# Two pairs of rooms for the readout matrices, and the skip weights added once at the end

## Chip, core and metric

The kernel runs on one core of a Trainium2 chip, in float32. The metric is the device time of one execution in microseconds (us). Each engine (PE for matrix products, DVE and ACT for elementwise work, POOL for elementwise work and the DMAs it issues, SP for the other DMAs) works through its own queue strictly in the order of that queue; between engines, instructions wait for one another through semaphores.

## What is computed

Two layers over 256 latent and 256 context tokens, width 1024. Layer 0 is attention and then a mixture of experts (MoE); layer 1 is a state-space mixer (SSM) in both directions, a gated linear unit and a second MoE; a final norm ends it. The change lies in the preparation of the SSM:

```
lbar = exp((a_re + i a_im) * dt)                  # 2 directions x 64 groups x 64 states
bb   = (lbar - 1) / (a_re + i a_im) * b           # input matrices, 16 channels a group
state_t = lbar * state_(t-1) + bb u_t             # both directions
y = Re(c . state), forward + backward             # readout matrices c
out = glu(gelu(y + d * u))                        # d: skip weights, one a channel
```

The kernel scans over chunks of four tokens. So it needs, for each group, `W` (powers of `lbar` times `bb`), readout matrices (powers of `lbar` times `c`, for the four places of a chunk) and within-chunk matrices (what the tokens of one chunk give to one another, to which the skip weights are added on the diagonal). All of these depend on weights alone.

## The kernel before

**Where the matrices are built.** `ssm_matrices` is a generator. It is run in slices ("asides") inside the expert loop of the first MoE, which streams 96 MB of expert weights. That loop goes over 16 pairs of experts, in steps: step k turns the gathered rows of pair k (`rows`: PE transposes at L329, copies to `xgT` at L1232 by ACT and DVE; POOL gathers the next pair's rows, L1180), turns the hidden values of pair k-2 (`hidT`, PE L1237, DVE copy to `hT` L1239), takes one aside, multiplies pair k-1 up (L1251, then `sg` on ACT L1259 and `hd` on DVE L1260) and pair k-2 down (L1277, ACT L1279, POOL L1280). The weights come in 1 MB tiles on SP's queue (L186). From step 4 on they go round eight tiles, and a tile is loaded again when PE has used it.

**What an aside does.** The 64 groups are taken eight at a time, q = 0 to 7, one a step (steps 4 to 11; the last matrices come in step 12). In the code's order an aside i is: `mats(i-1)`, `loadB(i+1)`, `coef(i)`, `readout(i)`, `loadC(i+1)`.

- `coef(q)` makes `W` on DVE: 13 operations with line L149, which is the line of the helper `InOrder`.
- `readout(q)` makes the readout matrices on DVE (L1607, L1608, L1609; twice each, for r = 0 and 1) and sends them with two DMAs on POOL's queue (L1611) to `Rd` in memory, whence they are fetched in layer 1. The result of r = 0 lies in `rooms[0]`, a half of `H1` (`H` in the profile), that of r = 1 in `rooms[1]`, a half of `b2` (`b`). The same two rooms serve every q. `cells` holds the `c` of two turns; it is loaded at L1578.
- `mats(q)` transposes `W` on PE (L1621, copied by ACT at L1623), multiplies it with `C` (`kp`, L1630), copies and transposes the product (`kt` L1633, `pk` L1635), and evacuates `pk` into `Kd`: one direction by ACT (L1638), the other by DVE with the skip weights `db` added (L1639).

**What sets the order.** A scheduler puts each engine's queue in order ahead of the run, by its own estimate of when each instruction can start; an instruction that stands later in the code can thus stand earlier in its queue. The operations called through `VP_` (all of `coef`) are tied, by the first lines quoted here, to stand behind the DVE instruction that precedes them in the code:

```
for p in reversed(nc.cur_bb.bb.instructions):
    if p is not i and p.engine == i.engine:
        tc.add_manual_dep(i, p.name, ...)
...
TE_ = InOrder(nc.tensor, 1)
P_, VP_, A_ = InOrder(nc.gpsimd, 3), InOrder(nc.vector, 1), InOrder(nc.scalar, 1)
```

For the first operation of `coef(i)` that is the addition L1639 of `mats(i-1)`. The operations of `readout` (`V_`) are not tied.

**Afterwards.** Later asides (steps 13 to 15) build the within-chunk matrices out of `Kd` with DMAs and POOL operations, and `shift` writes a few rows into `brow` by a DMA on SP's queue and has PE transpose them (L1545). `brow` is a tile of 128x512 that holds bias rows in attention and again in layer 1. The tile with the tag `gb` is another of that size, used for norm gains at the same places.

Of the kernel before, what the change touches and what calls it, by code (L numbers as in the profile page):

```python
# [10 lines left out]
F32 = mybir.dt.float32  # L11
# [119 lines left out]
def bc(ap, shape):  # L131
    return ap.to_broadcast(shape)
# [3 lines left out]
def hybrid(ctx: ExitStack, tc: tile.TileContext, A, out, taps=None, stop=None):  # L136
    nc = tc.nc
    taps = taps or {}
    V_ = nc.vector
# [29 lines left out]
    sm = ctx.enter_context(tc.tile_pool(name="sm", bufs=1))  # L169
# [3 lines left out]
    def bank(tag="b", name="bank"):  # L173
        return psp["p"].tile([128, 512], F32, tag=tag, bufs=psp[tag], name=name)
# [46 lines left out]
    brow = per.tile([128, 512], F32, name="brow")  # L221
# [52 lines left out]
    Rd = dram.tile([128, 2, 64, 64], F32, name="Rd")  # L274
# [529 lines left out]
    def dispatch_open(layer, Ht, M, VB, tag, xn2=None):  # L804
# [50 lines left out]
        def st(name, shape, dt=F32, bufs=1):  # L855
            return dp.tile([128] + list(shape), dt, tag=name, bufs=bufs, name=name)

        def logits(t):
            turn(HT[t % 2], Ht[t], 1)
            pl = bank(name="pl")  # L860
            for kk in range(8):
                for i in range(nt):
                    p = slice(64 * i, 64 * i + 64) if nt == 2 else slice(0, 128)
                    nc.tensor.matmul(pl[p, :36], lhsT=HT[t % 2][:, kk, p], rhs=rws[:, kk, i], start=kk == 0, stop=kk == 7)
            L = lr[:, 360 + 36 * t:396 + 36 * t] if layer else st("L", [36], bufs=2)
            V_.scalar_tensor_tensor(L, in0=pl[:, :36], scalar=xns[t], in1=C, op0=OP.mult, op1=OP.add)
            xns[t] = L
            if layer == 0 and t >= 2:
                nc.gpsimd.memset(M.xg[t % 2], 0.0)

        def choose(t):
            L = xns[t]
            gl, el = L[:, 0:4], L[:, 4:36]

# [651 lines left out]
    def cmul(eng, o, x, y, tm, neg=False):  # L1526

        eng.tensor_mul(tm[0], x[0], y[0])
        eng.tensor_mul(tm[1], x[1], y[1])
        eng.tensor_sub(o[0], tm[0], tm[1])  # L1530
        eng.tensor_mul(tm[0], x[0], y[1])
        eng.tensor_mul(tm[1], x[1], y[0])
        eng.tensor_add(o[1], tm[0], tm[1])
        if neg:
            eng.tensor_scalar(o[1], o[1], -1.0, 0.0, op0=OP.mult, op1=OP.add)
# [13 lines left out]
    def ssm_matrices(sctx):  # L1549
# [4 lines left out]
        Kd = H1[:, 0].rearrange("p (d g c) -> p d g c", d=2, c=16)  # L1554
        with ExitStack() as bctx:
            with ExitStack() as wctx:
                wq = wctx.enter_context(tc.tile_pool(name="ssmw", bufs=1))
                st = {}

                db = H1[:, 1, 0:512].rearrange("p (g c) -> p g c", c=16)  # L1560
                for h in range(2):
                    nc.gpsimd.dma_start(db[64 * h:64 * h + 64].rearrange("p g c -> p (g c)"),
                                        A["sd"][h:h + 1].to_broadcast([64, 512]))
                eye = wq.tile([128, 16], F32, name="eye")
                nc.gpsimd.tensor_add(eye, ident[:, 48:64], ident[:, 112:128])


                rooms = [t.rearrange("p (g t c) -> p g t c", t=4, c=16) for t in (H1[:, 1, 512:1024], b2[:, 512:1024])]
                cells = b2[:, 0:512].rearrange("p (i r g c) -> p i r g c", i=2, r=2, c=16)
                cb = M0[0].oh.rearrange("p a b c -> p (a b c)").rearrange("p (r g c) -> p r g c", r=2, c=16)  # L1570
                tm = [wq.tile([128, NG, 4, 16], F32, name=f"tm{i}") for i in range(2)]
                Bs, Cs = {}, {}

                def loadB(q):
                    if q < 64 // NG:
                        Bs[q] = wq.tile([128, 2, NG, 16], F32, tag="B", bufs=2, name="B")
                        nc.gpsimd.dma_start(Bs[q], A["sbq"][q])
                        nc.gpsimd.dma_start(cells[:, q % 2], A["sc"][:, :, q * NG:q * NG + NG, :])  # L1578

                def loadC(q):  # L1580
                    if q < 64 // NG:
                        Cs[q] = wq.tile([128, 2, NG, 32], F32, tag="C", bufs=2, name="C")
                        nc.gpsimd.dma_start(Cs[q], A["scq"][q])
                loadB(0)
                loadC(0)


                def coef(q):
                    gs = slice(q * NG, q * NG + NG)
                    B, C = Bs.pop(q), Cs.pop(q)  # L1590
                    VP_.tensor_scalar(C[:, 1], C[:, 1], -1.0, 0.0, op0=OP.mult, op1=OP.add)
                    W = wq.tile([128, 2, NG, 4, 16], F32, tag="W", bufs=2, name="W")
                    st[q] = C, W
                    cmul(VP_, (cb[:, 0], cb[:, 1]), [bc(CF[:, i, gs][:, :, None], [128, NG, 16]) for i in range(2)],
                         (B[:, 0], B[:, 1]), [t[:, :, 0, :] for t in tm])
                    cmul(VP_, (W[:, 0], W[:, 1]),
                         [bc(LX[:, :, i, gs].rearrange("p t g -> p g t")[:, :, :, None], [128, NG, 4, 16]) for i in range(2)],
                         [bc(cb[:, i][:, :, None, :], [128, NG, 4, 16]) for i in range(2)], tm)

                def readout(q):  # L1600

                    gs = slice(q * NG, q * NG + NG)
                    C = [bc(cells[:, q % 2, i][:, :, None, :], [128, NG, 4, 16]) for i in range(2)]
                    L = [bc(LR[:, :, i, gs].rearrange("p t g -> p g t")[:, :, :, None], [128, NG, 4, 16]) for i in range(2)]
                    for r in range(2):
                        x, y = rooms[r], tm[r]
                        V_.tensor_mul(x, L[0], C[r])  # L1607
                        V_.tensor_mul(y, L[1], C[1 - r])  # L1608
                        V_.tensor_tensor(x, x, y, op=OP.add if r else OP.subtract)  # L1609
                    for r in range(2):  # L1610
                        nc.gpsimd.dma_start(Rd[:, r, gs], rooms[r].rearrange("p g t c -> p g (t c)"))  # L1611

                def mats(q):
                    C, W = st.pop(q)
                    g0 = q * NG // 2
                    for i in range(0, NG // 2, 2):
                        pt = bank("vt", name="vt")
                        for k in range(2):
                            for r in range(2):
                                g = 2 * (i + k)  # L1620
                                nc.tensor.transpose(pt[:, (2 * k + r) * 128:(2 * k + r) * 128 + 128],  # L1621
                                                    W[:, r, g:g + 2].rearrange("p g a b -> p (g a b)"), ident)
                        nc.scalar.copy(VR[:, g0 + i:g0 + i + 2], pt.rearrange("p (k r b) -> p k r b", k=2, r=2))  # L1623

                    kp = bank("kp", name="kp")
                    for h in range(2):
                        for r in range(2):
                            for i in range(NG // 2):
                                g = 2 * i + h
                                nc.tensor.matmul(kp[32 * i:32 * i + 32, 64 * h:64 * h + 64], lhsT=C[:, r, g, :],  # L1630
                                                 rhs=W[:, r, g].rearrange("p a b -> p (a b)"), start=r == 0, stop=r == 1)
                    kt = wq.tile([128, 128], F32, tag="kt", bufs=1, name="kt")
                    nc.scalar.copy(kt, kp[:, 0:128])  # L1633
                    pk = bank("vt", name="pk")
                    nc.tensor.transpose(pk[:, 0:128], kt, ident)  # L1635
                    pd = pk[:, 0:128].rearrange("p (i d c) -> p d i c", d=2, c=16)
                    gs = slice(g0, g0 + NG // 2)
                    nc.scalar.copy(Kd[:, 1, gs], pd[:, 1])  # L1638
                    V_.tensor_add(Kd[:, 0, gs], pd[:, 0], db[:, gs])  # L1639
                n = 64 // NG  # L1640
                for i in range(n + 1):
                    if i:
                        mats(i - 1)
                    if i < n:
                        loadB(i + 1)
                        coef(i)
                        readout(i)
                        loadC(i + 1)
                        if not i:
                            nc.gpsimd.tensor_mul(db, db, bc(eye[:, None, :], [128, 32, 16]))  # L1650
                        yield
            yield

            sp2 = sctx.enter_context(tc.tile_pool(name="ssm2", bufs=1))
# [447 lines left out]
```

## Time and profile before

| what | value |
|---|---|
| median of three runs | 1202.22 us (1200.32 to 1202.37) |
| the profiled execution | 1193.77 us, span of its instructions 1192.0 us |
| PE, DVE, ACT, POOL busy in the span | 912.6, 625.3, 349.5, 268.6 us |
| expert loop of the first MoE | about 401 to 712 us of the span |
| asides with `coef`, `readout` and `mats` | 443 to 588 us of the span |

Lines are those of the kernel; H and b are the rooms. "Idle before" or "waited for" is time in which an engine had nothing to do until the named releaser was done. PEclk is the granted clock of PE as a share of 2.4 GHz; the DMA share is the mean busy share of the 16 DMA engines. A wait behind which a busy engine or a full DMA queue stands costs nothing by itself.

### The profile page before, as it was taken

What the parts mean: (1) busy time and instruction counts of PE and PEld (TensorE: products, weight loads), DVE (VectorE), ACT (ScalarE), POOL (GpSimd) and SP (SyncE); (2) the same over time, 40 slices, a digit from 0 to 9 for tenths busy, and PEclk for the clock granted to TensorE, in tenths of its full rate; (3) what the DMA queues carried; (4) which work ended last, traced back from release to release, by engine and by line L of the source; (5) the groups of instructions that cost most, each with busy time, mean ns of one, the idle gap of its engine ahead of it and who ended that gap; (6) DMA issues with size and microseconds to landing.
All of it is one profiled execution on the core that took longest, in us unless ns stands there. A gap on an engine that the chain in (4) does not pass through costs nothing. (4 is left out here: it accounts for less than half of the span.)

```text
span 1192.0 us, 15041 instructions
## 1 busy us (share of the span) xinstructions
PE 912.6 (77%) x5398; PEld 477.6 (40%) x5398; DVE 625.3 (52%) x1656; ACT 349.5 (29%) x705; POOL 268.6 (23%) x347
## 2 busy tenths in 40 slices
PE   3587989999897599676897896975189597676763
PEld 0375865444486333222342244732068442122110
DVE  1778794676549425555510028989947841111113
ACT  2332225666533212111220113622763320000001
POOL 0533331322324323121116305010035300000001
PEclk7788999999998699978999997987589798777896
DMA  9782222666744689978899974374257679999993
GB/s 287 267 214 71 71 71 71 213 230 222 269 170 194 226 336 410 416 270 304 334 422 350 409 302 142 143 283 156 97 198 272 247 318 420 420 420 419 420 420 142
DMA packets 54814, 317.14 MB, mean 266 GB/s; under 512 B 8587, under 2 KB 9627, under 8 KB 21712
## 3 DMA queue, kind: packets, MB, share of 16 engines
q1 hardware_dynamic: 42910, 285.49, 63.3%
q0 software_dynamic: 10080, 26.92, 6.1%
q10 hardware_dynamic: 1746, 3.73, 0.9%
q8 instruction: 44, 0.72, 0.2%
q14 instruction: 34, 0.28, 0.1%
HBM read 305.80 MB, written 19.94 MB: 273 GB/s over the span
## 5 line engine op out<-in xcount | busy, mean ns | idle before, releaser
L1251 PE MATMUL ph<-w,xgT 128*64 128x512 f32 x512 | 134.8, 640 | 9.6 <-DMA w<-in_gu 9.6
L248 PE MATMUL pm<-wmod,cs 128*32 128x512 f32 x352 | 51.8, 681 | 61.7 <-DMA wmod<-in_modw 53.5
L339 PE MATMUL pp<-wlo,xo 128*128 128x512 f32 (+1 forms) x224 | 88.5, 395 | 4.9 <-POOL wlo L360 4.8
L338 PE MATMUL pp<-whi,xo 128*128 128x512 f32 (+1 forms) x224 | 90.5, 405 | 1.3 <-ACT whi L358 1.3
L340 PE MATMUL pp<-whi,xo 128*128 128x512 f32 (+1 forms) x224 | 87.9, 393 | 0.0
L1277 PE MATMUL py<-w,hT 128*64 128x512 f32 x224 | 73.7, 623 | 5.2 <-DMA w<-in_dn 5.0
L1251 PEld LDWEIGHTS ph<-w,xgT 128*64 128x64 f32 x512 | 38.7, 144 | 82.5 <-issue 57.7
L360 POOL TENSOR_TENSOR wlo<-win,whi 128x1024 fp32r<-128x1024 f32 (+1 forms) x20 | 44.9, 2265 | 78.8 <-ACT whi L358 78.8
L1251 PE MATMUL ph<-w,xn 128*32 128x512 f32 x256 | 42.4, 747 | 24.7 <-DMA w<-in_gu 24.6
L1260 DVE TENSOR_TENSOR a<-a,ph 128x256 f32<-128x256 f32 x8 | 3.4, 421 | 98.8 <-ACT a L1259 98.8
L1260 DVE TENSOR_TENSOR hd<-sg,ph 128x256 f32<-128x256 f32 x16 | 6.7, 418 | 86.7 <-ACT sg L1259 86.7
L1303 PE MATMUL py<-w,m 128*32 128x512 f32 x256 | 43.8, 778 | 9.7 <-DMA w<-in_dn 8.5
L339 PEld LDWEIGHTS pp<-wlo,xo 128*128 128x128 f32 x224 | 44.8, 200 | 15.1 <-POOL wlo L360 7.3
L338 PEld LDWEIGHTS pp<-whi,xo 128*128 128x128 f32 x224 | 44.9, 201 | 10.2 <-ACT whi L358 2.2
L582 DVE TENSOR_REDUCE nm<-sc 128x1 f32<-128x512 f32 (+1 forms) x64 | 35.0, 551 | 26.1 <-PE sc L615 15.5
L340 PEld LDWEIGHTS pp<-whi,xo 128*128 128x128 f32 x224 | 44.4, 198 | 8.8
L248 PEld LDWEIGHTS pm<-wmod,cs 128*32 128x32 f32 x352 | 9.4, 116 | 89.6 <-issue 51.3
L1003 DVE SCALAR_TENSOR_TENSOR Yl<-py,WS,Yh 128x512 fp32r<-128x512 f32 x18 | 13.4, 750 | 56.2 <-ACT Yh L1002 43.5
L1251 PE MATMUL ph<-w,xg 128*32 128x512 f32 x256 | 33.2, 649 | 12.3 <-DMA w<-in_gu 11.0
L1259 ACT ACTIVATE sg<-ph 128x256 f32<-128x256 f32 x16 | 6.1, 383 | 124.0 <-PE ph L1251 122.3
L363 POOL TENSOR_TENSOR wlo<-glu,whi 128x512 fp32r<-128x512 f32 x16 | 26.7, 1697 | 67.5 <-ACT whi L358 65.1
L585 ACT ACTIVATE e<-sc,nm 128x512 f32<-128x512 f32 (+1 forms) x64 | 37.4, 586 | 12.7 <-DVE nm L582 8.4
(486 smaller groups left out, 1964.0 us busy)
## 6 DMA issues: line engine op xcount, KB each, us to landing
w<-in_gu SPq DMA_DIRECT2D x127, 1024.0 KB
w<-in_dn SPq DMA_DIRECT2D x62, 1024.0 KB
wmod<-in_modw SPq DMA_DIRECT2D x42, 1024.0 KB
win<-in_win SPq DMA_DIRECT2D x8, 1024.0 KB
glu<-in_glu SPq DMA_DIRECT2D x8, 1024.0 KB
yd<-in_zero SPq DMA_DIRECT2D x1, 4096.0 KB
wo<-in_wout SPq DMA_DIRECT2D x4, 1024.0 KB
w<-yd SPq DMA_DIRECT2D x4, 1024.0 KB
```

What stands on the lines that cost most here:

```text
L248: nc.tensor.matmul(pm[32 * i:32 * i + 32, :], lhsT=cs[:, kk, :], rhs=w(kk), start=kk < 4, stop=kk >= 4)
L338: nc.tensor.matmul(o, lhsT=lh, rhs=rh, start=start, stop=False)
L339: nc.tensor.matmul(o, lhsT=lh, rhs=rl, start=False, stop=False)
L340: nc.tensor.matmul(o, lhsT=ll, rhs=rh, start=False, stop=stop)
L360: self.engines[i].tensor_tensor(lw, w[:, 2 * i:2 * i + 2, :], hi.bitcast(F32), op=OP.subtract)
L363: e.tensor_tensor(lw[:, k], w[:, 2 * i + k, :], hi.bitcast(F32)[:, k], op=OP.subtract)
L582: V_.tensor_reduce(nm, sp_[:, :n], axis=AX.X, op=OP.max, negate=True)
L585: nc.scalar.activation(e[:, :n], sp_[:, :n], AF.Exp, bias=nm, scale=1.0, accum_out=z)
L1003: V_.scalar_tensor_tensor(Yl[:, s], in0=py, scalar=ws, in1=Yh[:, s].bitcast(F32), op0=OP.mult, op1=OP.subtract)
L1251: nc.tensor.matmul(ph[s, :], lhsT=st["x"][:, 4 * q + kk, s], rhs=g[:, i, kk % 2] if M.dma else g[:, i], start=(q, kk) == (0, 0), stop=(q, ...
L1277: nc.tensor.matmul(py[s, :], lhsT=st["hT"][:, fk, s], rhs=d[i][:, fk, hf * 512:hf * 512 + 512], start=fk == 0, stop=fk == 1)
L1303: nc.tensor.matmul(py[s, :], lhsT=st["hT"][:, fk, s], rhs=r, start=fk == 0, stop=fk == 1)
```

## The change

The readout matrices get a second pair of rooms: `brow` and a new tile `Rr` with the tag `gb`. Even q use the first pair, odd q the second. And ACT evacuates both directions of `pk` at once, without the skip weights; these are added to all 32 entries of `Kd[:, 0]` by one DVE operation after the last `mats`.

```
+                rooms += [t.rearrange("p (g t c) -> p g t c", t=4, c=16)
+                          for t in (brow, sm.tile([128, 512], F32, tag="gb", bufs=1, name="Rr"))]
...
+                    o = rooms[2 * (q % 2):2 * (q % 2) + 2]
                     for r in range(2):
-                        x, y = rooms[r], tm[r]
+                        x, y = o[r], tm[r]
                         V_.tensor_mul(x, L[0], C[r])
                         V_.tensor_mul(y, L[1], C[1 - r])
                         V_.tensor_tensor(x, x, y, op=OP.add if r else OP.subtract)
                     for r in range(2):
-                        nc.gpsimd.dma_start(Rd[:, r, gs], rooms[r].rearrange("p g t c -> p g (t c)"))
+                        nc.gpsimd.dma_start(Rd[:, r, gs], o[r].rearrange("p g t c -> p g (t c)"))
...
-                    nc.scalar.copy(Kd[:, 1, gs], pd[:, 1])
-                    V_.tensor_add(Kd[:, 0, gs], pd[:, 0], db[:, gs])
+                    nc.scalar.copy(Kd[:, :, gs], pd)
...
                         yield
+                V_.tensor_add(Kd[:, 0], Kd[:, 0], db)
             yield
```

## Rows read from the trace of the kernel before

**Rows 1.** Chain that ended last, in order of time: start us, us, what.
```profile
964.27 16.77 DMA w<-in_dn
...
1141.91 19.89 DMA w<-in_gu
```

**Rows 2.** Windows: stretch, its us, busy us (x count) by engine, PEclk, DMA share, GB/s.
```profile
440.00:520.00 80.00, 65.95 (x400) 26.05 (x396) 43.83 (x94) 15.96 (x33) 20.22 (x28) 0.94 1.01 409
520.00:600.00 80.00, 61.97 (x357) 23.67 (x358) 44.34 (x91) 14.37 (x31) 16.01 (x21) 0.89 0.80 293
600.00:700.00 100.00, 84.85 (x346) 29.99 (x345) 10.64 (x19) 13.57 (x23) 33.31 (x70) 0.98 1.02 394
```

**Rows 3.** Waits of DVE from 440 to 600 us: total us, times, longest.
```profile
DVE H L1607 <- DMA Rd<-H: 32.0, 6, 7.9
DVE H L1639 <- ACT H L1638: 16.5, 4, 6.7
...
DVE b L1607 <- DMA Rd<-b: 4.2, 5, 1.4
```

**Rows 4.** Waits of PE in the same stretch.
```profile
PE vt L1621 <- DVE W L149: 24.7, 8, 8.3
```

**Rows 5.** Timeline of the longest PE wait: start us, us, engine, instruction, [idle before].
```profile
533.46 0.60 POOL L1611 DMA_DIRECT2D Rd<-H  x1
...
536.36 0.22 DVE L1639 TENSOR_TENSOR H<-pk,H 128x64 f32<-128x64 f32 x1 [6.73 <-ACT H L1638]
...
542.60 0.69 DVE L1607 TENSOR_TENSOR H<-LR,b 128x512 f32<-128x512 f32 x1 [5.42 <-DMA Rd<-H]
...
548.00 0.45 PE L1621 MATMUL vt<-cst,W 128*128 128x128 f32 x1 [8.35 <-DVE W L149]
```

**Rows 6.** Timeline of PE: transposes that open steps 4, 8, 11 and 12.
```profile
441.58 1.09 PE L329 MATMUL pt<-cst,xg 128*128 128x128 f32 x8
...
518.76 1.09 PE L329 MATMUL pt<-cst,xg 128*128 128x128 f32 x8
...
595.35 1.09 PE L329 MATMUL pt<-cst,xg 128*128 128x128 f32 x8
...
607.09 1.09 PE L329 MATMUL pt<-cst,xg 128*128 128x128 f32 x8
```

**Rows 7.** Groups by line, 440 to 600 us: shape, count, busy us, mean ns, idle before.
```profile
L1621 PE MATMUL vt<-cst,W 128*128 128x128 f32 x64 | 12.6, 301 | 25.4 <-DVE W L149 24.7 <-ACT Vm L1623 0.4
...
L1630 PE MATMUL kp<-W,C 128*32 128x64 f32 x256 | 8.4, 240 | 0.0
...
L1609 DVE TENSOR_TENSOR H<-H,tm 128x512 f32<-128x512 f32 x8 | 5.5, 683 | 0.0
...
L1635 PE MATMUL pk<-cst,kt 128*128 128x128 f32 x8 | 2.6, 329 | 2.7 <-ACT Vm L1623 2.7
...
L1633 ACT COPY kt<-kp 128x128 f32<-128x128 f32 x8 | 2.1, 267 | 0.3 <-PE kp L1630 0.3
...
L1639 DVE TENSOR_TENSOR H<-pk,H 128x64 f32<-128x64 f32 x8 | 1.8, 220 | 16.5 <-ACT H L1638 16.5
```

**Rows 8.** Line L1611, the 16 DMAs to Rd: time from issue to landing.
```profile
DMA to landing us min/median/max: 4.2/8.5/11.0
```

**Rows 9.** Timeline of DVE: L1607 hoisted, and `coef` against the `hT` copy.
```profile
401.13 0.69 DVE L1607 TENSOR_TENSOR H<-LR,b 128x512 f32<-128x512 f32 x1 [1.94 <-DVEq L1047]
...
460.39 0.69 DVE L1607 TENSOR_TENSOR H<-LR,b 128x512 f32<-128x512 f32 x1 [7.87 <-DMA Rd<-H]
...
560.29 0.41 DVE L1239 COPY hT<-pt 128x256 f32<-128x256 f32 x1
```

**Rows 10.** Timeline near the last matrices: POOL, PE, DVE.
```profile
586.12 0.57 POOL L1611 DMA_DIRECT2D Rd<-b  x1
...
589.85 0.27 PE L1545 MATMUL bt<-cst,brow 64*128 64x64 f32 x1
...
594.17 0.42 DVE L1260 TENSOR_TENSOR hd<-sg,ph 128x256 f32<-128x256 f32 x1 [5.61 <-ACT sg L1259]
```

## The prediction

> **What bounds the kernel now.** The chain that ended last comes first. From 964 us to the end it consists of weight loads of the second MoE, some 20 us a link [rows 1]. It says what holds the last fifth; what lies before it is shifted as a whole if an earlier stage ends sooner, since those loads begin only when the SSM's last part asks for them. So the question is whether the first MoE, where the changed code runs, ends sooner.
>
> The windows tell what bounds that stage [rows 2]. From 440 to 520 us and from 600 to 700 us the DMA share is 1.01 and 1.02: transfers bound it, and no engine can make it faster there. From 520 to 600 us the share is 0.80 with 293 GB/s instead of 409: 0.20 x 80 = 16 us of the transfer time are lost. Loads stop when no tile of the ring has been freed, and PE frees them. So PE is late there, although it is not at its limit: it is busy 62 of 80 us, at a granted clock of 0.89.
>
> Why PE is late: its largest wait is for `W`, made by DVE, 24.7 us in 8 waits [rows 4]. And DVE's own waits in this stretch are of the kinds that the diff touches [rows 3]: 36.2 us (32.0 + 4.2) at L1607, where the next readout may not write into a room before the DMA out of it has landed, and 16.5 us at L1639, which waits for PE and ACT to finish the matrices of the turn before. Together 52.7 us. Both stand in DVE's queue ahead of `coef` or within it, so `W` comes late. The longest case shows the whole chain [rows 5]: L1639 ends 6.73 us of idling at 536.36; the DMA issued at 533.46 holds L1607 until 542.60, a further 5.42 us, with most of `coef` behind it; PE gets its `W` at 548.00 after 8.35 us of nothing. The transpose behind the wait takes 0.45 us against a mean of 0.30 [rows 5, 7], so the lower clock after the idling makes PE later still.
>
> **The change, part by part.**
>
> *Two pairs of rooms.* L1607 of turn i now has to wait for the DMA of turn i-2. Its 16 DMAs land 4.2 to 11.0 us after issue, 8.5 at the median [rows 8]; a turn takes 19.3 us or more (below). If L1607 stays where it is in the code's order, the 36.2 us go to nothing. The bound on the other side is 36.2 us kept: L1607 is not tied to its place, and the trace shows it far ahead, at 401.13, four steps before its aside, and at 460.39 ahead of the copies of step 5, as soon as the scheduler thinks the room free [rows 9]. With two pairs it can be put one turn further ahead and stand at the same wait. I take the larger part as gone or harmless: even where L1607 of turn i+2 stands in front of the next step's copies, it is no longer in the middle of a `coef` that is already due.
>
> The Trainium skill ("DMA: Bandwidth & Descriptors", section "Anatomy of one DMA — SWDGE (gpsimd) path") gives such a transfer 2.0 us plus its bytes over 436 GB/s, an estimated 2.6 us for these 256 KB. By that figure the rooms would be free almost at once, and a second pair would save next to nothing. The trace does not agree: 8.5 us at the median, with the transfer engines full [rows 8, 2].
>
> *The addition L1639.* Eight DVE operations of 0.22 us go (1.8 us), and with them 16.5 us of waiting. Added are one DVE operation of 128x512 (as L1609: 0.68 us) and, on ACT, a copy twice as wide; the 128x128 copy `kt` takes 0.27 us, so all eight together cost less than 2.1 us [rows 7]. ACT is busy 14.4 us of the 80 [rows 2], which hides it. The new addition waits for the last copy as the last L1639 did, near 588 us; behind it DVE has nothing until `hd` at 594.17 [rows 10]. Without that cover it costs its 0.68 us once.
>
> *What is moved.* The first operation of `coef(i)` was tied behind L1639 of the matrices before; now the nearest DVE instruction ahead of it in the code is the `hT` copy of its own step. It can no longer run ahead of its step. Before, it could: `coef` of turn 5 followed L1639 at 536.36, while the `hT` copy of that step came at 560.29 [rows 5, 9]. Price: nothing, if `W` comes before PE reaches the matrices; at most a wait like the longest, 8.35 us, in each of eight steps.
>
> *The borrowed tiles.* `brow` is written by `shift` through SP's queue. That write must now follow the last DMA out of `brow`, issued at 586.12 and landing by 597 at the latest; PE used its result at 589.85, so this step moves back some 8 us [rows 8, 10]. Nobody needs it before layer 1, but SP's weight loads stand behind it: 0 us while loads already issued keep the transfer engines full, at most 11 us if none are. I take 0, since the share is 1.02 after 600 us [rows 2]. `gb` has no other user until layer 1.
>
> *The sum.* Two ways. First, the lost transfer time: 16 us, if PE frees tiles in time throughout. Second, the pace: steps 4 to 8 took 518.76 - 441.58 = 77.2 us with the transfers full, 19.3 us a step; steps 8 to 12 took 607.09 - 518.76 = 88.3 us [rows 6]. At the first pace the saving is 11.1 us. PE can hold that pace: a step without matrices and without waits takes 607.09 - 595.35 = 11.7 us [rows 6], the matrices (12.6 + 8.4 + 2.6) / 8 = 3.0 us [rows 7], together 14.7, which leaves 4.6 us a step. Between 11.1 and 16 I take 12, near the lower, because some of the L1607 waits will be kept. After 600 us the transfers are full again, so nothing is won there and nothing given back; the 12 us go through to the end.
>
> The profiled execution took 1193.8 us, 8.4 less than the median of the runs, so it would be 1181.8 after; against the median of 1202.2 the forecast is **1190.2 us**.
>
> **Rivals.**
>
> *The wait only moves one turn ahead.* L1607 is put forward until it meets the same landing, and only L1639's share of the waits goes: 16.5 / 52.7 = 31%, of 16 us some 5 us: 1197. For it: the hoisted places of rows 9. Against: the costliest waits come where the two meet, as in rows 5, and the second is harmless without the first.
>
> *Slower: PE waits for `W` in every step.* `coef` is now tied to its step behind the `hT` copy, while the scheduler may still put the transposes of `W` early in PE's queue. What a step can bear is the 4.6 us of slack. To eat up also the 16 us that are lost today (2.0 us a step over eight steps) the wait must reach 6.6 us in each; from there it decides. At the longest wait seen, 8.35 us, it is 8 x 1.75 = 14 us slower: 1216. For it: rows 9. Against: from L1607 at 542.60, with most of `coef` behind it, to PE's start at 548.00 it is 5.4 us [rows 5], and PE has 11.7 us of expert work in a step to do meanwhile.
>
> *No change.* The late tiles are not due to DVE, or SP stands still behind the write into `brow` for the full 11 us and takes back what was won: 1201 to 1203. Against it stands rows 5.
>
> **Chances.** What a measurement of this kernel can tell from no change is about 0.2%, 2.4 us. The forecast (a saving of 8 to 18 us): 0.55. The moved wait (2.4 to 8 us): 0.20. No change: 0.08. Slower: 0.17. That makes faster 0.75, same 0.08, slower 0.17. The range runs from 1184 us, 18 us less, where the whole 16 us and a little of the lower clock's cost come back, to 1204 us, which takes in the moved wait and no change; what is left out is mostly the slower case.
>
> **What would show it.** Right: L1639 gone; waits of L1607 for `Rd` well under 36 us, or standing where DVE has nothing else; PE's waits for `W` under 10 us in total; a DMA share of 0.95 or more in the 80 us after step 8 begins; steps 8 to 12 at about 19 to 20 us; the stages after the first MoE of unchanged length. Wrong: PE waiting for `W` some 7 us in each step; L1607 still idle 30 us with PE late behind it; a gap in SP's loads at `shift`; or a later stage that changed its length because the scheduler put its queues in another order.

## The result, and the profile after

| | before | after |
|---|---|---|
| median | 1201.27 us (4 runs, 1197.32 to 1202.37) | 1181.61 us (4 runs, 1179.77 to 1182.61) |
| profiled execution | 1193.77 us | 1182.01 us |

The ratio is 0.9845, 95% interval 0.9816 to 0.9874: 1.5% faster, 18.6 us of the 1202.2 that the forecast started from, where 12 were forecast. The median of 1181.61 us lies 2.4 us below 1184 us, the fast end of the range. A second comparison, below, gave 0.9877 (0.9843 to 0.9911). The medians of the table lie 19.7 us apart, the two profiled executions only 11.8 us: the one of before was 8.4 us faster than the median that the forecast started from, the one of after was at its median.

The gain lies in the expert loop. SP's two DMAs at L280 follow the loop in both kernels; this is the view of that line of before:

```profile
L280 SPq DMA_DIRECT2D a<-md x2: 487/538/588, 709.6 to 710.2; - x2
```

And of after:

```profile
L280 SPq DMA_DIRECT2D a<-md x2: 483/536/588, 697.9 to 698.4; - x2
```

They start 11.7 us earlier, and from there to the end of the span it is 1192.0 - 709.6 = 482.4 us before and 1180.2 - 697.9 = 482.3 us after.

The windows of after (columns as in [rows 2]):

```profile
440.00:520.00 80.00, 66.96 (x405) 26.86 (x403) 45.86 (x97) 15.70 (x33) 21.92 (x30) 0.94 1.01 409
520.00:600.00 80.00, 68.80 (x381) 25.29 (x378) 41.51 (x81) 15.16 (x31) 16.89 (x21) 0.91 0.89 348
600.00:700.00 100.00, 87.62 (x349) 32.80 (x348) 13.79 (x23) 14.72 (x26) 33.92 (x71) 0.97 0.97 369
```

In the second window the DMA share rose from 0.80 to 0.89, so by the share 8.8 us of transfer time are lost there instead of 16. It did not reach the 1.02 of full queues. The last column says more: at the 409 GB/s of the first window, the 293 GB/s of before mean (1 - 293/409) x 80 = 22.7 us lost, and the 348 GB/s of after 11.9 us. The difference, 10.8 us, is close to the 11.7 us by which the loop ends earlier; that of the shares, 7.2 us, is not. (The 0.97 of the third window is the loop's end: in slices of 10 us the share is 1.01 to 1.03 up to 690 us and 0.56 in the last.) What DVE waited for from 440 to 600 us:

```profile
DVE brow L1610 <- DMA Rd<-brow: 25.0, 3, 11.3
DVE H L1610 <- DMA Rd<-H: 21.0, 3, 9.3
...
DVE Rr L1610 <- DMA Rd<-Rr: 3.5, 3, 1.2
DVE b L1610 <- DMA Rd<-b: 2.9, 2, 1.5
DVE H L1654 <- ACT H L1641: 1.0, 1, 1.0
```

The waits for rooms (L1610 is L1607 of before) did not go: they are 52.4 us, against the 36.2 of [rows 3]. The 16.5 us at the addition went; the one that is left (L1654) waits 1.0 us. So DVE idles at these two places as long as before, 53.4 us against 52.7. PE, in the same stretch:

```profile
PE pt L1237 <- DVE hd L1260: 9.4, 4, 4.3
PE vt L1624 <- DVE W L149: 8.3, 3, 4.1
```

Its wait for `W` fell from 24.7 us [rows 4] to 8.3 us. Its wait for `hd` rose; in before it was:

```profile
PE pt L1237 <- DVE hd L1260: 2.9, 2, 1.5
```

So what PE waits for DVE fell from 27.6 us in all to 17.7 us, while DVE idles as long as before. Where the waits for rooms stand is in the timeline of DVE (start us, us, engine, instruction, [idle before]):

```profile
450.11 0.41 DVE L1260 TENSOR_TENSOR hd<-sg,ph 128x256 f32<-128x256 f32 x1
457.85 0.69 DVE L1610 TENSOR_TENSOR H<-LR,b 128x512 f32<-128x512 f32 x1 [7.33 <-DMA Rd<-H]
458.46 0.68 DVE L1232 COPY xgT<-pt 128x512 f32<-128x512 f32 x1
459.06 0.41 DVE L1239 COPY hT<-pt 128x256 f32<-128x256 f32 x1
459.39 0.28 DVE L149 TENSOR_SCALAR C<-C 128x256 f32<-128x256 f32 x1
...
467.69 0.69 DVE L1612 TENSOR_TENSOR Rr<-Rr,tm 128x512 f32<-128x512 f32 x1
468.29 0.41 DVE L1260 TENSOR_TENSOR hd<-sg,ph 128x256 f32<-128x256 f32 x1
475.51 0.69 DVE L1610 TENSOR_TENSOR brow<-LR,b 128x512 f32<-128x512 f32 x1 [6.81 <-DMA Rd<-brow]
...
535.92 0.69 DVE L1610 TENSOR_TENSOR H<-LR,b 128x512 f32<-128x512 f32 x1 [9.28 <-DMA Rd<-H]
...
538.69 0.41 DVE L1260 TENSOR_TENSOR hd<-sg,ph 128x256 f32<-128x256 f32 x1
...
560.03 0.69 DVE L1610 TENSOR_TENSOR brow<-LR,b 128x512 f32<-128x512 f32 x1 [11.30 <-DMA Rd<-brow]
...
562.48 0.41 DVE L1260 TENSOR_TENSOR hd<-sg,ph 128x256 f32<-128x256 f32 x1
```

At 467.69 the readout of turn 1 is finished in the second pair. The write at 475.51 is that of turn 3, into the same room: it has been put two turns ahead, in front of the copies of the next step, and waits for the DMA out of that room to land. The same place of the queue was taken by turn 1 at 460.39 in before [rows 9]; in after turn 2 stands there, at 457.85. A room is used again as soon as the order thinks it free, with one pair or with two. The two longest waits, 9.28 and 11.30 us, stand in front of `hd` as well: PE's longest waits for `hd`, 4.30 and 3.39 us, end at 539.16 and 562.95, right behind the `hd` of 538.69 and 562.48. PE's opening transposes in after:

```profile
439.56 1.09 PE L329 MATMUL pt<-cst,xg 128*128 128x128 f32 x8
...
515.23 1.09 PE L329 MATMUL pt<-cst,xg 128*128 128x128 f32 x8
...
582.31 1.09 PE L329 MATMUL pt<-cst,xg 128*128 128x128 f32 x8
...
599.63 1.09 PE L329 MATMUL pt<-cst,xg 128*128 128x128 f32 x8
```

Steps 8 to 12 took 599.63 - 515.23 = 84.4 us, 21.1 each: better than the 88.3 of [rows 6], and not the 19.3 of the full queues.

### The profile page after: what moved, and what is told of

The parts are those of the page before. It is cut to its first block, busy times and chain, and to the rows that moved or that the text cites. A ratio compares the mean times of both kernels' runs of the same rounds, so it can differ in the third digit from the quotient of the medians.

```text
span 1180.2 us, 15033 instructions
## 1 busy us (share of the span) xinstructions
PE 913.9 (77%) x5398; PEld 477.3 (40%) x5398; DVE 625.1 (53%) x1649; ACT 350.4 (30%) x705; POOL 270.7 (23%) x347
## 5 line engine op out<-in xcount | busy, mean ns | idle before, releaser
L1251 PE MATMUL ph<-w,xgT 128*64 128x512 f32 x512 | 140.9, 629 | 10.0 <-DMA w<-in_gu 10.0
L1277 PE MATMUL py<-w,hT 128*64 128x512 f32 x224 | 76.7, 646 | 0.9 <-DMA w<-in_dn 0.8
L363 POOL TENSOR_TENSOR wlo<-glu,whi 128x512 fp32r<-128x512 f32 x16 | 26.7, 1698 | 69.4 <-ACT whi L358 67.1
L1277 PEld LDWEIGHTS py<-w,hT 128*64 128x64 f32 x224 | 22.1, 146 | 43.5 <-issue 40.4
```

The lines of the kernel that those rows point to most:

```text
L363: e.tensor_tensor(lw[:, k], w[:, 2 * i + k, :], hi.bitcast(F32)[:, k], op=OP.subtract)
L1251: nc.tensor.matmul(ph[s, :], lhsT=st["x"][:, 4 * q + kk, s], rhs=g[:, i, kk % 2] if M.dma else g[:, i], start=(q, kk) == (0, 0), stop=(q, ...
L1277: nc.tensor.matmul(py[s, :], lhsT=st["hT"][:, fk, s], rhs=d[i][:, fk, hf * 512:hf * 512 + 512], start=fk == 0, stop=fk == 1)
```

## Experiments

Theories stood at the start. By the first (A in the expectations), the whole gain comes from taking the addition out of DVE's queue, and the waits for rooms that remain still cost time. By its rival (B), the gain is that of the second pair; by a third (C), the waits that remain cost nothing. D and E are told where they are tested. Unless a sentence says otherwise the diffs are against the changed kernel, and ratios are to the kernel before.

**The changed kernel and the kernel before, once more.**

> The changed kernel once more, for a tighter interval and a second execution to read. If the median's gain is steady, the ratio is 0.982 to 0.988 (1179 to 1187 us). If the 11.8 us between the two profiled spans are nearer to the truth than the 19.7 us between the medians, the ratio is 0.989 to 0.992.

0.9877 (0.9843 to 0.9911); median 1181.07 us against 1196.18 (23 runs, 1191.29 to 1203.07). Waits for rooms 50.6 us, PE's wait for `W` 9.5 us, DMA share 0.93 in the second window. The result repeats, at 14.7 us (1 - 0.9877, of 1196.18).

> A second profile of the kernel before. If the spread of its runs (1191 to 1203 us) comes from the expert loop, its transfer share from 520 to 600 us differs from the 0.80 of the first profile in the direction of its time, some 1 us for each 0.0125 of the share, and the rest of the span has the same length within 1 us. If it comes from elsewhere, the share is the same.

1198.92 us. Its second window:

```profile
520.00:600.00 80.00, 59.27 (x344) 22.43 (x344) 43.17 (x87) 13.69 (x29) 16.23 (x21) 0.85 0.72 270
```

The first of PE's waits in 440 to 600 us:

```profile
PE vt L1621 <- DVE W L149: 25.7, 8, 9.1
```

The share is 0.72, not the 0.80 of [rows 2]: 0.28 x 80 = 22.4 us of transfer time lost, 6.4 more than in the execution on which the prediction was built; by the bytes it is 27.2 us, 4.5 more. About half of the 5.1 us between the two executions lies outside the loop (the loop's end 2.8 us later, the rest 2.3 longer), which was not expected.

**Two pairs of rooms alone** (the addition back in each turn):

```
-                    nc.scalar.copy(Kd[:, :, gs], pd)
+                    nc.scalar.copy(Kd[:, 1, gs], pd[:, 1])
+                    V_.tensor_add(Kd[:, 0, gs], pd[:, 0], db[:, gs])
...
-                V_.tensor_add(Kd[:, 0], Kd[:, 0], db)
```

> Only the second pair of rooms; the addition stays in each turn, on DVE. Theory A (all of the gain comes from taking the addition out of DVE's queue; the scheduler puts the first write to a room one turn further ahead, to the same landing): the waits for Rd stay above 30 us, the waits of the addition stay near 16 us, and the time is 1195 to 1204 us, a ratio of 0.995 to 1.003. Theory B (two pairs of rooms shorten the turn): the waits for Rd fall under 15 us and the time is 1182 to 1192 us.

0.9973 (0.9948 to 0.9998), median 1193.43 us: 3 us. DVE's waits:

```profile
DVE H L1642 <- ACT H L1641: 17.1, 5, 6.1
DVE brow L1610 <- DMA Rd<-brow: 14.8, 3, 6.9
DVE H L1610 <- DMA Rd<-H: 11.6, 2, 7.3
...
DVE H L1610 <- DMA b<-in_sc: 8.0, 1, 8.0
```

And the first of PE's waits:

```profile
PE vt L1624 <- DVE W L149: 25.5, 7, 9.9
```

The addition is L1642 here. The waits at those writes stay (37.8 us with the 8.0 for `cells` and 3.4 at the second rooms), and so does PE's wait for `W`. This profiled execution, 1200.58 us, was the slowest of its twelve. A second pair by itself is worth next to nothing.

**The addition at the end alone** (one pair):

```
-                rooms += [t.rearrange("p (g t c) -> p g t c", t=4, c=16)
-                          for t in (brow, sm.tile([128, 512], F32, tag="gb", bufs=1, name="Rr"))]
...
-                    o = rooms[2 * (q % 2):2 * (q % 2) + 2]
+                    o = rooms[0:2]
```

> Only the addition at the end; one pair of rooms as before. Theory A: 1180 to 1187 us, a ratio of 0.982 to 0.988, with waits for Rd as long as in the changed kernel (about 50 us in all) and waits of PE for W of 10 us or less. Theory B: 1195 us or more, with W late as before.

0.9935 (0.9910 to 0.9960), median 1188.05 us. DVE's waits at the rooms:

```profile
DVE H L1608 <- DMA Rd<-H: 44.6, 6, 10.6
DVE H L1608 <- issue: 9.0, 1, 9.0
DVE b L1608 <- DMA Rd<-b: 7.9, 6, 1.5
```

And PE's two largest:

```profile
PE pt L1237 <- DVE hd L1260: 11.0, 4, 4.2
PE vt L1622 <- DVE W L149: 8.9, 3, 4.6
```

DVE stands still at the rooms for 61.5 us, in seven turns, more than in any other kernel here (9.0 us of it, at turn 7's write, have no releaser in the profile); yet PE's wait for `W` is 8.9 us, as low as with both parts. So it was the addition's place that passed the waits on to `W`. By way of `hd` they still reach PE, with 11.0 us. The time is just outside the 1180 to 1187 us that the first theory expected: the addition alone does not bring the whole gain. In the same comparison the changed kernel, which has the second pair besides, is 7.0 us faster (1181.07).

> Only the addition at the end, once more, on the chip of the two others. Theory D: seven waits, some 60 us, 1185 to 1190 us, slower than both. Rival E: within 2 us of the second pair for the last turn alone.

0.9912 (0.9882 to 0.9942), median 1188.36 us, waits for rooms 63.7 us in seven turns. The same.

**The changed kernel with the readout tied to its place.** The six operations of `readout` are called through `VP_`, so that none can be put ahead of the `coef` before it. Nothing else changes:

```
-                        V_.tensor_mul(x, L[0], C[r])
-                        V_.tensor_mul(y, L[1], C[1 - r])
-                        V_.tensor_tensor(x, x, y, op=OP.add if r else OP.subtract)
+                        VP_.tensor_mul(x, L[0], C[r])
+                        VP_.tensor_mul(y, L[1], C[1 - r])
+                        VP_.tensor_tensor(x, x, y, op=OP.add if r else OP.subtract)
```

> The changed kernel with the six operations of readout tied to their place in the code, so that they cannot be put ahead. Theory A says that the 52 us of waits at the rooms are still there and still cost what transfer time is lost between 510 and 570 us, about 10 us by the shares: with them gone (under 5 us) the time is 1170 to 1176 us, a ratio near 0.976. Rival C (the waits stand where DVE has nothing else and cost nothing): waits gone, time as in the changed kernel, 1180 to 1184 us.

0.9794 (0.9759 to 0.9829), median 1171.07 us. All of DVE's waits of 440 to 600 us:

```profile
DVE hd L1260 <- ACT sg L1259: 42.0, 9, 12.6
DVE xgT L1232 <- PE pt L329: 27.4, 9, 5.2
```

PE waits for weights instead of for DVE; the first of its waits:

```profile
PE py L1277 <- DMA w<-in_dn: 8.1, 9, 2.0
```

And the second window is full:

```profile
520.00:600.00 80.00, 70.30 (x379) 26.59 (x376) 38.03 (x75) 15.63 (x31) 15.34 (x19) 1.00 1.02 418
```

DVE waits as long as in the kernel before (69.4 us against 68.2 in all), but only for work that follows from PE, and PE waits neither for `W` nor for `hd`. Transfers bound the stretch, and PE's granted clock in it is 1.00 (0.89 before). The waits for rooms that the changed kernel keeps do cost time: some 10 us.

**One pair, the addition at the end, the readout tied** (the last two edits together).

> One pair of rooms, the addition at the end, readout tied to its place in the code. If a room is in time as soon as nothing writes to it before its turn comes (a turn is some 19 us, a landing 8 to 12), the second pair is not needed: waits for Rd under 5 us, 1168 to 1175 us, as with two pairs and the tie. If two pairs are needed too, waits for Rd of 20 us or more and 1180 us or above.

0.9778 (0.9748 to 0.9809), median 1171.45 us; no wait for a room, share 1.02. With the readout in its place the second pair is not needed.

**The kernel before with the readout tied, and nothing else.** The same three lines with `rooms[r]` as before; the tied writes appear under L149, the helper's line.

> The kernel before with nothing changed but the tie of readout: one pair of rooms and the addition in each turn. If the two waits of DVE add up, the room waits go and those of the addition stay at some 16 us: 1180 to 1187 us. If the early writes were the larger part of it, 1172 to 1179 us. If the addition alone keeps W late, 1190 us or more.

0.9784 (0.9756 to 0.9812), median 1171.50 us. DVE's waits at the addition and the rooms:

```profile
DVE H L1639 <- ACT H L1638: 15.8, 6, 3.7
...
DVE H L1639 <- issue: 3.8, 1, 3.8
DVE b L149 <- DMA Rd<-b: 1.1, 1, 1.1
DVE H L149 <- DMA Rd<-H: 0.4, 1, 0.4
```

And the first of PE's:

```profile
PE vt L1621 <- DVE W L149: 6.3, 5, 1.7
```

The addition waits as long as before, and it does no harm: the second window's share is 1.02. The profiled execution, 1182.06 us, was the slowest of its seven (the fastest was 1169.03); its steps from 3 on began some 5 us later than in before (435.21 against 429.89 us), for a reason ahead of the changed code that I did not find.

**The addition in eight parts again, but behind the readout of its step** in the code, so that it stands ahead of no `coef` that is due:

```
                         loadC(i + 1)
+                    if i:
+                        ks = slice((i - 1) * NG // 2, i * NG // 2)
+                        V_.tensor_add(Kd[:, 0, ks], Kd[:, 0, ks], db[:, ks])
+                    if i < n:
...
-                V_.tensor_add(Kd[:, 0], Kd[:, 0], db)
```

> The changed kernel with the addition split again into eight, one in each turn, but behind readout in the code, so that coef is not tied to it. If what cost time was where the addition stood (in front of coef, which waits with it), this is as fast as the changed kernel, 1178 to 1185 us. If eight waits of DVE for ACT cost time wherever they stand, it is 1187 us or more.

0.9873 (0.9838 to 0.9908), median 1180.83 us: the changed kernel's time. The addition waits 7.5 us in the stretch. So not the eight operations were dear, but their place in front of `coef`. One rival is left without a run of its own: that it helps when ACT alone empties `pk`, instead of ACT and DVE. Against it, the view of L1639 in before names nothing that waited for that addition.

**The second pair for some turns only.** Is the second pair worth one wait less (six instead of seven), whichever turn has it? In the first kernel turn 7 alone uses it; in the second turns 3 and 7 do:

```
-                    o = rooms[2 * (q % 2):2 * (q % 2) + 2]
+                    o = rooms[2 * (q == 7):2 * (q == 7) + 2]
```

The second kernel has this line in its place:

```
+                    o = rooms[2 * (q in (3, 7)):2 * (q in (3, 7)) + 2]
```

> The changed kernel with the second pair of rooms used by the last turn alone. Theory D: a second pair does not shorten a wait, it saves one. With one pair there is a wait behind each of turns 0 to 6, seven; with two pairs in turn the last write put ahead is that of turn 7, behind turn 5, so six. Here too it is six, none behind turn 6: some 52 us of waits, 1178 to 1185 us, as the changed kernel. Rival E (the alternation itself gives each DMA more time): as with one pair, 1186 to 1191 us, and about 60 us of waits.

0.9890 (0.9855 to 0.9924), median 1183.46 us; waits behind six turns, 48.6 us together, none of them behind turn 6. Of these, 7.8 us are not for a room: turn 7's early write waits for the load of `cells`.

> The second pair used by turns 3 and 7 alone. Theory D: no wait behind turns 3 and 6, five waits, some 43 us, and between the changed kernel and the tied ones: 1173 to 1178 us. Rival E (alternation): between one pair and the changed kernel, 1182 to 1190 us.

0.9840 (0.9802 to 0.9878), median 1181.56 us (1171.83 to 1183.26); waits behind five turns, 39.1 us, of which 12.9 us are for `cells`. The ratio falls with the number of waits (0.9912, 0.9890, 0.9840), but the intervals overlap and the median lies between what the two theories expected: that each wait is worth the same isn't settled.

## Why the prediction came out as it did

- **What bounds the stage: right.** PE late for want of `W` and transfers lost from 520 to 600 us; where the readout is tied, the share is 1.02 and 1171 us come out. (Beside its landing times the prediction calls the transfer engines full; from 520 to 600 us they were not, at 0.80.)
- **"I take the larger part as gone or harmless": wrong in what did it.** Nothing went: the waits grew from 36.2 to 52.4 us. The order put the write one turn further ahead and met the same landing, as the first rival said and [rows 9] showed. Most of it did become harmless, but through the addition: with two pairs alone PE still waits 25.5 us for `W`, with the addition alone 8.9. And not all of it was harmless: the write left the middle of `coef`, as the prediction says, but it now stands in front of `hd`, for which PE waits 9.4 us instead of 2.9, and the tie, which ends this, gives a further 10 us.
- **The addition: right that it goes and costs nothing at its new place, far too small in worth.** The eight wide copies took 8 x 0.267 = 2.1 us on ACT, at the bound, and the final addition waited 1.0 us. But its price was taken as a share of DVE's waits, 31% or 5 us. Alone it brought 0.65% to 0.88%, some 8 to 11 us. Shares of waiting were the wrong measure, since the two kinds work upon each other: `W` comes late, so PE's matrices, ACT's copies and the addition come late, and the addition holds the next `coef`, which makes the next `W`. Taking either out of that circle is enough to bring PE's wait for `W` under 10 us (8.9 without the addition, 6.3 without the waits for rooms), which is what the runs show; only without the waits for rooms does the wait for `hd` go as well (11.0 us in the one, none in the other). That the delay goes round in this way is read from the order of the queues.
- **"16 us of the transfer time are lost": the term that was mis-sized.** It was read from the DMA share; the bytes of the same row give 22.7 us. In the two profiled executions of before and the two of after the bytes lost come to 22.7, 27.2, 11.9 and 8.6 us, a gain of 10.8 to 18.6 us, and the loop ends at 709.6, 712.4, 697.9 and 694.2 us, a gain of 11.7 to 18.2. The shares give 16, 22.4, 8.8 and 5.6 us, a gain of 7.2 to 16.8 only. By the ratios 18.6 and 14.7 us were measured. With one pair, the addition at the end and the tie the loop ended at 686.9 us, 22.7 us earlier than in the execution on which the prediction was built. The 16 was also taken from one execution and set against a median 8.4 us slower; later comparisons gave 1196.2 to 1198.3 us for that median. The fast end of the range, a saving of 18 us, was built on the 16, and a larger saving was given no chance; the second comparison lies within it, the first just beyond.
- **`coef` tied behind the `hT` copy, price nothing: right.** Where the waits for rooms are gone as well, no wait of PE for `W` is left. The slower rival wanted 6.6 us a step; in after three waits came to 8.3 us.
- **The write into `brow` on SP, price 0: right.** It moved far more than the 8 us: the write was issued at 623.8 us, where in before it was at 324.3, and PE's product from it (L1545) came at 653.39 instead of 589.85. Yet SP waited 1.1 us at L1541 in all, and that for weights and `hd`, and the DMA share stayed at 1.01 or more up to 690 us.

These are SP's waits of after from 600 to 660 us:

```profile
SPq L186 <- DMA w<-in_gu: 16.7, 4, 4.8
...
SPq L1541 <- DMA w<-in_dn: 0.8, 1, 0.8
...
SPq L1541 <- DVE hd L1260: 0.3, 1, 0.3
```

- **The rest passes through: right,** 482.4 and 482.3 us behind the loop (481.4 to 486.1 in all thirteen profiled executions).
- **The tests named ahead:** PE's waits for `W` under 10 us, yes; waits for rooms well under 36 us, a share of 0.95 and steps of 19 to 20 us, no (52.4, 0.89, 21.1). They said rightly that half of the fault was still there.

Open: why executions of the kernel before lie between 1190.5 and 1203.7 us; the reason for the late steps in the profiled execution of the tied kernel before; and what a single wait for a room is worth.

The best version is the kernel before with those six operations tied, with or without the change: 1171.07, 1171.45 and 1171.50 us, 2.1% to 2.2% faster than before and some 10 us faster than the changed kernel. The three can't be told apart.

## What to carry to other kernels

- Before giving a producer a second buffer, see where its first write stands in the queue. If the order puts it forward to wherever the buffer seems free, a second buffer is met by the same landing; putting the write back into its place costs no memory and gave more here.
- Don't price waits by their share of an engine's idle time. 52.7 and 53.4 us of idling on DVE went with 27.6 and 17.7 us of PE waiting for DVE: follow each wait to what stands behind it, above all an operation that waits for a consumer's result in front of the producer's next turn.
- Work out a sum from more than one execution where their spread is near the gain, and lost transfer time from the bytes moved, not only from the busy share of the transfer engines.

## What was not expected of the hardware

How soon the fastest of the DMAs out of the rooms lands goes with how full the transfer engines are; the median does not. The view of L1614 of after ([rows 8] for before):

```profile
DMA to landing us min/median/max: 7.4/9.3/12.1
```

In the three executions whose second window had a share of 0.72 to 0.80 (the two of before, and two pairs alone) the shortest landing took 4.0 to 4.6 us; in the ten others, with shares of 0.85 to 1.02, 6.3 to 7.7 us. The medians, 7.3 to 9.6 us, don't follow the share. What links the two was not tested. The Trainium skill ("DMA: Bandwidth & Descriptors", section "Anatomy of one DMA — SWDGE (gpsimd) path") would give an estimated 2.6 us; no run here shows a landing that short.

The busy share of the transfer engines can be high while they move less. In the second windows of the four executions of before and after the shares are 0.72, 0.80, 0.89 and 0.93, the bytes 0.66, 0.72, 0.85 and 0.89 of those of the first window.

Two executions of one program can differ by 6.4 us in lost transfer time (by the share) within the same 80 us, with PE's waits for `W` almost alike (24.7 and 25.7 us). Its waits for `hd` were 2.9 and 5.9 us and its granted clock 0.89 and 0.85, so the waits for `W` alone don't tell how much of a late tile is paid in transfers.
